# Grouped attention by head pairs and half tokens, the convolution's layer norm behind it, and lo of that stage's weights made by adding transfers

## The chip, the cores and the metric

The kernel runs on one core of a Trainium2 chip. The metric is the device time of one execution in microseconds (us), lower is better. The kernel of before takes 1296.93 us (median of three runs, 1295.86 to 1297.26).

## The reference

Two transformer blocks in float32 on 512 tokens of width 1024. The first has a pooling mixer and a stick-breaking attention with 16 heads. The second, which the change touches, has a mixer of two parallel branches, then cross attention to 256 memory tokens, then a gated feed-forward net. Cut to what matters here:

```python
def parallel_mixer(h, ...):            # h: 512 x 1024
    z = h @ w_in                       # 512 + 512 for the convolution, 512 for q, 128 + 128 for k and v
    a = a_val * sigmoid(a_gate)
    a = silu(layernorm(dwconv_centred(a, conv_dw, conv_dw_b), conv_ln_g, conv_ln_b))   # 31 taps, 512 channels
    q = apply_axial_rope(rmsnorm(q, q_norm_g))    # 8 heads of 64
    k = apply_axial_rope(rmsnorm(k, k_norm_g))    # 2 heads of 64, each for four heads of q
    att = softmax(q k^T / 8) v
    return concatenate([a, att]) @ w_out
```

Behind it stand a residual with its norm, and the cross attention, whose keys and values (`mem_n @ w_mem_kv`) depend on the memory alone.

## The kernel before

**Products in three parts.** Operands are split as x = hi + lo, both float32r, and each product is three matmuls, hi*hi + hi*lo + lo*hi (`mm3`, line 149). A weight tile of 128 x 1024 is loaded from SP's queue into a raw buffer (three of them, line 183), ACT copies it to hi (`wh`) and DVE subtracts to lo (`wl`) (`weights`, lines 186 to 193); wh and wl have four buffers each. Matmuls with plain float32 operands (transposes, products with v, memory keys and values) are single.

**The stage.** `pair(j)` (line 865) makes value and gate of 128 channels of the convolution, `tokens` (line 238) the queries, lines 884 to 894 keys and values. `conv_steps` (line 811) gives DVE 30 taps per channel group, 120 in all, then the layer norm: sums, mean by a matmul, squares, second matmul, scaling. These steps are paced: `catch_up` (line 125) gives out taps as long as DVE's counted time over `CONV_RATE` is behind PE's counted time.

**The attention.** `gqa_scores(n_)` (line 956) makes one head's scores against 512 keys for four blocks of 128 tokens, twelve products with 64 rows of contraction, and its softmax (line 917): maximum on DVE, exponential and sum on ACT, reciprocal on DVE, scaling on ACT. `turn_p` transposes the probabilities on PE, ACT copies them out. After every second head eight products with v give two heads' output (lines 982 to 989). `fill` (line 256) puts steps of the memory keys (`mem_k_steps`) and values (`mem_v_steps`) in between as work for PE. After the loop the rest of the taps and the norm are given out, then follow fillers, the first halves of four tiles of w_out2 with the attention's output (lines 999 to 1005), silu and split of the convolution, and `post_norm` (line 1022) with the second halves. `fill(1000)` at line 1123 gives out the fillers that are left. PSUM has eight banks, all from one pool. Instructions of one engine run in the order in which a compile-time planner lays them out; it starts from the order of the program and moves ahead what is ready.

**For comparison**, the first attention's scores (`score_products`, line 561) alternate the two heads of a pair, whose operands lie in partitions 0 to 63 and 64 to 127; its products with v (`unit_out`, line 622) are 512, 384, 256 and 128 columns wide.

The lines that set the old order, quoted:

```python
        for q in range(4):
            ps = PS("sc")
            qs_ = slice(q * P, q * P + P)
            mm3(ps, qh[r, qs_], ql[r, qs_], kh[r], kl[r], True, True)
```

Of the kernel before, what the change touches and what calls it, by code (L numbers as in the profile page):

```python
# [18 lines left out]
P = 128  # L19
# [12 lines left out]
RATES = (0.5, 0.6)  # L32
TAIL = 1.0
AHEAD = 3
CONV_RATE = 0.87
FILL_A = 2.5
FILL_B = 1.5
FILL_C = 4.0


VEC = {}
# [24 lines left out]
def tile_kernel(ctx: ExitStack, tc: tile.TileContext, A, out):  # L66
# [6 lines left out]
    up_scope = ExitStack()  # L73
    up = up_scope.enter_context(tc.tile_pool(name="up", bufs=2))

    uid = [0]

    def nm(s):
# [14 lines left out]
    def PS(name="ps"):  # L93
        return pp.tile([P, S], F32, tag="ps", name=nm(name))
# [47 lines left out]
    def mm(o, l, r, start, stop):  # L142
        nc.tensor.matmul(o, l, r, start=start, stop=stop, skip_group_check=True)  # L143
# [5 lines left out]
    def mm3(o, lh, ll, rh, rl, start, stop):  # L149
        mm(o, lh, rh, start, False)  # L150
        mm(o, lh, rl, False, False)
        mm(o, ll, rh, False, stop)
        back["pe"] += 3 * o.free_size() / 2400.0
        catch_up()
# [7 lines left out]
    def V(name, j=0):  # L162
        c = VEC[name] + j
        return vec[:, c:c + 1]
# [21 lines left out]
    def weights(src, n=1024):  # L186
        raw = raw_weights(src, n)
        hi = wp.tile([P, 1024], F32R, tag="wh", name=nm("wh"))
        lo = wp.tile([P, 1024], F32R, tag="wl", name=nm("wl"))
        ins = (act(hi[:, :n], raw[:, :n], AF.Copy), tt(lo[:, :n], raw[:, :n], f(hi[:, :n]), ALU.subtract))  # L190
        while before:
            tc.add_manual_dep(ins[len(before) - 1], before.pop(), NOSYNC, reason="order of arrival")
        return hi, lo

    def dense(srcs, xsp):

        KT = len(xsp)
        ws = [weights(src, KT * P) for src in srcs]
        ps = [PS() for _ in srcs]
        for k in range(KT):  # L200
            c = slice(k * P, k * P + P)
            for p_, (wh, wl) in zip(ps, ws):
                mm3(p_, wh[:, c], wl[:, c], xsp[k][0], xsp[k][1], k == 0, k == KT - 1)
        return ps
# [8 lines left out]
    def scaled_weights(src, gain, k0, n):  # L213

        raw = raw_weights(src)
        hi = wp.tile([P, 1024], F32R, tag="wh", name=nm("wh"))
        lo = wp.tile([P, 1024], F32R, tag="wl", name=nm("wl"))
        for i in range(1024 // n):
            c, g = slice(i * n, i * n + n), V(gain, k0 + i)
            act(hi[:, c], raw[:, c], AF.Copy, scale=g)  # L220
            stt(lo[:, c], raw[:, c], g, f(hi[:, c]), ALU.mult, ALU.subtract)
        return hi, lo
# [15 lines left out]
    def tokens(src, gain, xsp, h, mid=None):  # L238

        pv = [PS() for _ in range(4)]  # L240
        for k in range(KD):
            if k % 2 == 0:
                wh, wl = scaled_weights(src[h * 4 + k // 2], gain, k, S) if gain else weights(src[h * 4 + k // 2])
            c = slice(k % 2 * S, k % 2 * S + S)
            for t in range(4):
                tk = slice(t * P, t * P + P)
                mm3(pv[t], xsp[k][0][:, tk], xsp[k][1][:, tk], wh[:, c], wl[:, c], k == 0, k == KD - 1)
                weave(0.68)
            if k == 4 and mid is not None:
                mid()  # L250
        return pv
# [260 lines left out]
    def evac_split(ps, g=None, n=S):  # L512
        hi, lo = G2(n)
        if g is None:
            act(hi, ps, AF.Copy)
            tt(lo, ps, f(hi), ALU.subtract)
        else:
            act(hi, ps, AF.Copy, scale=g)
            stt(lo, ps, g, f(hi), ALU.mult, ALU.subtract)
        return hi, lo  # L520
# [247 lines left out]
    xs, hsp = ple(1, xs, xsp, pl, n4, "mix_pre", mem_normed)  # L768


    mk = []
    mv = [[None, None], [None, None]]


    def mem_k_steps():
        for m in range(KD):
            raw = raw_weights(A["w_mem_k"][m])
            ps = PS()
            for k in range(KD):
                mm(ps[:, :M_MEM], raw[:, k * P:k * P + P], mem[k], k == 0, k == KD - 1)  # L780
                step_pe(0.43)
                yield 0.43
            mk.append(evac_split(ps[:, :M_MEM], None, M_MEM))

    def mem_v_steps(h):
        pv = [PS() for _ in range(2)]
        for kk in range(4):
            raw = raw_weights(A["w_mem_v"][h * 4 + kk])
            for k2 in range(2):
                k = 2 * kk + k2  # L790
                for t in range(2):
                    mm(pv[t], mem[k][:, t * P:t * P + P], raw[:, k2 * S:k2 * S + S], k == 0, k == KD - 1)
                step_pe(1.7)
                yield 1.7
        for t in range(2):
            mv[t][h] = evac_split(pv[t])


    conv = []
# [11 lines left out]
    def conv_steps():  # L811
        for j in range(4):
            while len(conv) <= j:
                yield 0.1
            av, cv = conv[j]
            for kk in range(31):
                d = 15 - kk
                if d == 0:
                    continue
                lo, hi = max(0, -d), min(S, S - d)  # L820
                stt(cv[:, lo:hi], av[:, lo + d:hi + d], V("conv_dw", 31 * j + kk), cv[:, lo:hi],
                    ALU.mult, ALU.add)
                yield 0

        cvs = [c[1] for c in conv]
        acc = G(name="ca")
        tt(acc, cvs[0], cvs[1], ALU.add)
        for j in (2, 3):
            tt(acc, acc, cvs[j], ALU.add)
        yield 3.0  # L830
        psm = PS()
        mm(psm, mean2, acc, True, True)
        acc = G(name="ca")
        for j in range(4):
            tt(cvs[j], cvs[j], psm, ALU.subtract)
            sq = acc if j == 0 else G(name="csq")
            act(sq, cvs[j], AF.Square)
            if j:
                tt(acc, acc, sq, ALU.add)
            yield 0  # L840
        yield 3.0
        psv = PS()
        mm(psv, mean2, acc, True, True)
        RC = rsqrt_(psv)
        yield 1.0
        for j in range(4):
            tt(cvs[j], cvs[j], RC, ALU.mult)
            yield 0

    def rotated(x, t, n, which):  # L850

# [11 lines left out]
        return o  # L863

    def pair(j):
        return dense([A["w_in2"][j], A["w_in2"][4 + j]], hsp)

    back.update(pe=0.0, dve=0.0, rate=CONV_RATE, steps=None)
    p0 = pair(0)
# [13 lines left out]

    pkv = [PS() for _ in range(2)]
    for kk in range(2):
        wh, wl = weights(A["w_kv2"][kk])
        for k4 in range(4):
            k = 4 * kk + k4
            c = slice(k4 * 256, k4 * 256 + 256)
            for t in range(4):  # L890
                o = pkv[t // 2][:, (t % 2) * 256:(t % 2) * 256 + 256]
                tk = slice(t * P, t * P + P)
                xh, xl = hsp[k][0][:, tk], hsp[k][1][:, tk]
                mm3(o, xh, xl, wh[:, c], wl[:, c], k == 0 and t % 2 == 0, k == KD - 1)
# [58 lines left out]
                outs.append(o)  # L953
        return outs

    def gqa_scores(n_):
        j, hd = n_ // 2, n_ % 2
        qh, ql = q2[j]
        r = slice(64 * hd, 64 * hd + 64)
        sc = []  # L960
        for q in range(4):
            ps = PS("sc")
            qs_ = slice(q * P, q * P + P)
            mm3(ps, qh[r, qs_], ql[r, qs_], kh[r], kl[r], True, True)
            sc.append(ps)
        return softmax(sc, S, *(x.rearrange("p (t h) -> p h t", t=4)[:, n_] for x in (qfac[:, :32], nqfac)))

    nqfac = negative(qfac[:, :32], 32)

    queue.append(mem_k_steps())  # L970
    queue.append(mem_v_steps(0))
    att = []
    pts = []
    cur = gqa_scores(0)
    fill(4)
    for n_ in range(8):
        nxt = gqa_scores(n_ + 1) if n_ < 7 else None
        fill(FILL_A)
        pts.append(turn_p(cur, S, False))
        fill(FILL_B)  # L980
        if n_ % 2:
            po = PS("o")
            for i in range(4):
                for hd in range(2):
                    mm(po[64 * hd:64 * hd + 64], v2[:, i * P + 64 * hd:i * P + 64 * hd + 64], pts[hd][i],
                       i == 0, i == 3)
            back["pe"] += 3.6
            catch_up()
            att.append(evac_split(po))
            pts = []  # L990
        cur = nxt

    for _ in back["steps"] or ():
        pass
    back["steps"] = None
    queue.append(mem_v_steps(1))
    fill(FILL_C)

    NW = 4
    wo = [weights(A["w_out2"][m]) for m in range(NW)]  # L1000
    wps = [PS() for _ in range(NW)]
    for m in range(NW):
        for k in range(4):
            c = slice(k * P, k * P + P)
            mm3(wps[m], wo[m][0][:, c], wo[m][1][:, c], att[k][0], att[k][1], k == 0, False)
    csp = []
    for j in range(4):
        c = conv[j][1]
        act(c, c, AF.Silu, scale=V("ln_g", j), bias=V("ln_b", j))
        csp.append(split(c))  # L1010

    def mixed(m):
        if m >= NW:
# [3 lines left out]
            mm3(wps[m], wo[m][0][:, c], wo[m][1][:, c], csp[k][0], csp[k][1], False, k == 3)  # L1017
        return wps[m]

    HALF = [slice(0, S // 2), slice(S // 2, S)]  # L1020

    def post_norm(mk_ps, half_ps, nhalf, gname, xs, done, at=1, ahead=()):

# [81 lines left out]
    def dense_halves(srcs, xsp):  # L1105
# [4 lines left out]
        for h in range(2):  # L1110
            for k in range(KD):
                c = slice(k * P, k * P + P)
                for p_, (wh, wl) in zip(ps, ws):
# [7 lines left out]
    xs = post_norm(mixed, half_steps([A["w_out2"][6], A["w_out2"][7]], att + csp), 2, "mix_post", xs,  # L1121
                   half_split(hsp, "mem_pre"), ahead=[A["w_mem_q"][m] for m in range(AHEAD)])
    fill(1000)


    mo = []
# [255 lines left out]
```

## Time and profile before

| | us |
|---|---|
| median of three runs | 1296.93 |
| the profiled execution | 1295.55 |
| its span, first to last instruction | 1293.8 |
| PE busy | 1273.2 |
| DVE busy | 850.9 |
| ACT busy | 659.0 |
| POOL busy | 4.2 |

Engines are PE (matmuls), DVE (vector), ACT (scalar activations), POOL (GpSimd) and SP (transfers). Times in a view count from the start of the span. Busy times of engines overlap, so they don't add up to the span; a wait on an engine matters only where the chain that ends last runs through it. A matmul's shown length overlaps with the next one's start; the distance between starts is its price. One float32 product appears as two instructions. What lies around the span, 1.75 us here, belongs to the time of the execution.

### The profile page before, as it was taken

The numbers are of one execution on the slowest core, as the hardware profiler recorded it, in microseconds if no ns is written. First come the engines' busy times: TensorE is split into PE (matmuls) and PEld (weight loads), VectorE is DVE, ScalarE is ACT, GpSimd is POOL, SyncE is SP. The second block draws the span as 40 slices with busy tenths as digits, with TensorE's granted clock in tenths as the row PEclk, the third lists the DMA queues.
The fourth block names the chain that finished last, engine by engine and source line by source line (L and its number), as shares of the span: only waits on it lengthen the run. The fifth ranks groups of instructions, "written<-read, shape, count | busy, mean of one in ns | idle before, by whom it ended". The sixth has DMA issues, their size and how long they took to land.

```text
span 1293.8 us, 16129 instructions
## 1 busy us (share of the span) xinstructions
PE 1273.2 (98%) x6228; PEld 1030.6 (80%) x6228; DVE 850.9 (66%) x1369; ACT 659.0 (51%) x1081; POOL 4.2 (0%) x46
## 2 busy tenths in 40 slices
PE   8999999999999999999999999999999999999997
PEld 6888888877777678888777488888988888888886
DVE  6885455587687744869999746543768877773223
ACT  6434344577675543543477755464545544442221
POOL 0000000000000000000000000000000000000000
PEclk9999999999999999999999999999999999999999
DMA  6323234212121243322122243301133333333321
GB/s 230 111 90 120 97 117 133 94 53 79 58 89 37 79 166 99 106 82 82 49 66 65 79 136 111 99 33 70 62 117 98 98 98 96 98 90 105 91 74 65
DMA packets 38957, 120.37 MB, mean 93 GB/s; under 512 B 4448, under 2 KB 8160, under 8 KB 38880
## 3 DMA queue, kind: packets, MB, share of 16 engines
q1 hardware_dynamic: 38880, 119.34, 29.2%
q8 instruction: 49, 0.80, 0.3%
q14 instruction: 28, 0.23, 0.1%
HBM read 115.12 MB, written 4.19 MB: 92 GB/s over the span
## 4 chain that ended last, share of the span: by engine, by line
PE 96%; DVE 2%; ACT 1%; issue 0%; DMA 0%; SPq 0%; DVEq 0%; ACTq 0%
PE ps L143 85%; PE o L143 3%; PE sc L143 3%; PE y L143 2%; PE pT L157 1%; PE aT L157 1%; PE ps L157 1%; DVE z L134 0%; ACT aT L113 0%; ACT hi L113 0%; DVE yg L134 0%; ACT wh L113 0%; DVE og L134 0%; DMA vec<-in_vec_dram 0%; DVE kp L588 0%
## 5 line engine op out<-in xcount | busy, mean ns | idle before, releaser
L143 PE MATMUL ps<-hi,wh 128*128 128x512 f32 (+1 forms) x1390 | 524.6, 378 | 6.2 <-ACT hi L349 5.0
L143 PE MATMUL ps<-lo,wh 128*128 128x512 f32 (+1 forms) x1390 | 519.7, 374 | 0.0
L143 PE MATMUL ps<-hi,wl 128*128 128x512 f32 (+1 forms) x1390 | 518.8, 373 | 0.0
L134 DVE TENSOR_TENSOR wl<-wr,wh 128x1024 fp32r<-128x1024 f32 (+2 forms) x160 | 191.1, 1197 | 179.2 <-ACT wh L113 172.9
L113 ACT ACTIVATE wh<-wr 128x1024 fp32r<-128x1024 f32 (+2 forms) x160 | 165.3, 1039 | 280.5 <-PE ps L143 182.5
L143 PEld LDWEIGHTS ps<-hi,wh 128*128 128x128 f32 x1390 | 262.4, 189 | 55.5 <-ACT hi L349 5.7
L143 PEld LDWEIGHTS ps<-lo,wh 128*128 128x128 f32 x1390 | 262.5, 189 | 47.4 <-DVE lo L350 1.5
L143 PEld LDWEIGHTS ps<-hi,wl 128*128 128x128 f32 x1390 | 262.3, 189 | 46.4 <-DVE wl L134 0.4
L143 PE MATMUL ps<-wh,hi 128*128 128x512 f32 (+1 forms) x256 | 100.4, 392 | 0.0
L143 PE MATMUL ps<-wh,lo 128*128 128x512 f32 (+1 forms) x256 | 96.6, 377 | 0.0
L143 PE MATMUL ps<-wl,hi 128*128 128x512 f32 (+1 forms) x256 | 96.5, 377 | 0.0
L139 DVE SCALAR_TENSOR_TENSOR cv<-aval,vec,cv 128x497 f32<-128x497 f32 (+14 forms) x120 | 84.8, 738 | 1.5 <-ACT cv L113 0.9
L139 DVE SCALAR_TENSOR_TENSOR wl<-wr,vec,wh 128x512 fp32r<-128x512 f32 (+1 forms) x80 | 48.5, 641 | 29.4 <-ACT wh L113 29.3
L139 DVE SCALAR_TENSOR_TENSOR fc<-fu,vec,fc 128x511 f32<-128x511 f32 x88 | 64.4, 748 | 4.0 <-ACT fc L113 2.9
L113 ACT ACTIVATE wh<-wr,vec 128x512 fp32r<-128x512 f32 (+1 forms) x80 | 47.1, 641 | 35.2 <-PE ps L143 22.5
L143 PEld LDWEIGHTS ps<-wh,hi 128*128 128x128 f32 x256 | 48.2, 188 | 10.6 <-issue 2.6
L143 PEld LDWEIGHTS ps<-wh,lo 128*128 128x128 f32 x256 | 48.2, 188 | 9.1
L143 PEld LDWEIGHTS ps<-wl,hi 128*128 128x128 f32 x256 | 48.3, 189 | 7.7 <-issue 0.2
L588 DVE TENSOR_TENSOR_SCAN kp<-kp,begin 128x383 f32<-128x383 f32 (+2 forms) x64 | 49.7, 809 | 6.4 <-ACT kp L113 6.1
L134 DVE TENSOR_TENSOR fu<-ps,R 128x512 f32<-128x512 f32 x44 | 29.4, 686 | 23.3 <-PE ps L143 23.1
L134 DVE TENSOR_TENSOR sq<-sq,sq 128x512 f32<-128x512 f32 (+1 forms) x58 | 38.0, 655 | 5.9 <-ACT sq L113 4.2
L113 ACT ACTIVATE fc<-fu,vec 128x512 f32<-128x512 f32 x44 | 34.7, 809 | 10.4 <-DVE fu L134 10.0
(163 smaller groups left out, 1316.9 us busy)
## 6 DMA issues: line engine op xcount, KB each, us to landing
wr<-in_w_up_dram SPq DMA_DIRECT2D x44, 512.0 KB, 3.5
wr<-in_ple_gate_dram SPq DMA_DIRECT2D x16, 512.0 KB, 3.5
wr<-in_w_down_dram SPq DMA_DIRECT2D x16, 512.0 KB, 3.6
wr<-in_a_w_in_dram SPq DMA_DIRECT2D x14, 512.0 KB, 3.6
wr<-in_a_w_out_dram SPq DMA_DIRECT2D x8, 512.0 KB, 3.5
wr<-in_w_k_dram SPq DMA_DIRECT2D x8, 512.0 KB, 3.6
wr<-in_b_w_q_dram SPq DMA_DIRECT2D x8, 512.0 KB, 3.5
wr<-in_w_v_dram SPq DMA_DIRECT2D x8, 512.0 KB, 3.5
```

The source lines that it names most:

```text
L113: ins = nc.scalar.activation(o, i, fn, **kw).ins
L134: ins = nc.vector.tensor_tensor(o, a, b, op).ins
L139: nc.vector.scalar_tensor_tensor(o, a, s, b, op0, op1)
L143: nc.tensor.matmul(o, l, r, start=start, stop=stop, skip_group_check=True)
L157: nc.tensor.transpose(o, i, ident)
L588: nc.vector.tensor_tensor_scan(o, o, begin[:, :n - 1], 0.0, ALU.mult, ALU.add)
```

## The change

`gqa_scores(j, g)` now does two heads (pair j) for two blocks of tokens (half g), alternating the heads in each of the three parts; one reciprocal serves all four blocks. `gqa_turn` transposes such a unit, `gqa_out` multiplies it with v, 256 columns wide, one unit later, right behind the next scores. The layer norm of the convolution leaves the paced steps and becomes `conv_norm`, with four stops behind the attention. Memory keys and values are first copied out plainly and split later (`mem_split`); three filler steps move from the end of the stage to a new place (`FILL_D`). For the stage's fourteen weights `added_weights` makes lo as -raw on ACT and lets a transfer from POOL's queue add the raw weights from DRAM to it. The taps' pace goes from 0.87 to 0.76.

```diff
-CONV_RATE = 0.87
+CONV_RATE = 0.76
+FILL_D = 4.0
...
+    def added_weights(src, n=1024):
+
+        raw = raw_weights(src, n)
+        hi = wp.tile([P, 1024], F32R, tag="wh", name=nm("wh"))
+        lo = wp.tile([P, 1024], F32R, tag="wl", name=nm("wl"))
+        act(hi[:, :n], raw[:, :n], AF.Copy)
+        act(lo[:, :n], raw[:, :n], AF.Copy, scale=-1.0)
+        nc.gpsimd.dma_start(lo[:, :n], src, accum_op=ALU.add)
+        return hi, lo
...
-            mk.append(evac_split(ps[:, :M_MEM], None, M_MEM))
+            if m % 2 == 0:
+                mk_raw.append(G(name="mkr"))
+            act(mk_raw[-1][:, m % 2 * M_MEM:m % 2 * M_MEM + M_MEM], ps[:, :M_MEM], AF.Copy)
...
+    def mem_split():
+
+        while mk_raw:
+            t = mk_raw.pop(0)
+            for i in range(2):
+                mk.append(split(t[:, i * M_MEM:i * M_MEM + M_MEM], M_MEM))
+        for t, h in list(mv_raw):
+            mv[t][h] = split(mv_raw.pop((t, h)))
...
+    def conv_norm():
+
         cvs = [c[1] for c in conv]
         acc = G(name="ca")
         tt(acc, cvs[0], cvs[1], ALU.add)
         for j in (2, 3):
             tt(acc, acc, cvs[j], ALU.add)
-        yield 3.0
+        yield
...
         psv = PS()
         mm(psv, mean2, acc, True, True)
         RC = rsqrt_(psv)
-        yield 1.0
         for j in range(4):
             tt(cvs[j], cvs[j], RC, ALU.mult)
-            yield 0
+            act(cvs[j], cvs[j], AF.Silu, scale=V("ln_g", j), bias=V("ln_b", j))
+            csp.append(split(cvs[j]))
+        yield
...
     def pair(j):
-        return dense([A["w_in2"][j], A["w_in2"][4 + j]], hsp)
+        return dense([A["w_in2"][j], A["w_in2"][4 + j]], hsp, added_weights)
...
+    def gqa_scores(j, g):
         qh, ql = q2[j]
...
+        sc = [[PS("sc") for _ in range(2)] for _ in range(2)]
+        for q in range(2):
+            qc = slice((2 * g + q) * P, (2 * g + q + 1) * P)
+            for n_, (a, b) in enumerate(((qh, kh), (qh, kl), (ql, kh))):
+                for hd in range(2):
+                    r = slice(64 * hd, 64 * hd + 64)
+                    mm(sc[hd][q], a[r, qc], b[r], n_ == 0, n_ == 2)
...
+        nc.vector.reciprocal(sm, sm)
+        for n_ in range(4):
+            act(pr[n_], pr[n_], AF.Copy, scale=sm[:, n_:n_ + 1])
+        return pr
...
+    def gqa_out(n_, pts):
+        g = units[n_][1]
+        if g == 0:
+            po[0] = PS("o")
+        for i in range(4):
+            for hd in range(2):
+                mm(po[0][64 * hd:64 * hd + 64, HALF[g]], v2[:, i * P + 64 * hd:i * P + 64 * hd + 64],
+                   pts[4 * hd + i][1], i == 0, i == 3)
+        step_pe(1.8)
+        if g:
+            att.append(evac_split(po[0]))
...
     for n_ in range(8):
-        nxt = gqa_scores(n_ + 1) if n_ < 7 else None
+        nxt = gqa_scores(*units[n_ + 1]) if n_ < 7 else None
+        if late is not None:
+            gqa_out(n_ - 1, late)
         fill(FILL_A)
-        pts.append(turn_p(cur, S, False))
+        late = gqa_turn(cur)
         fill(FILL_B)
...
+    csp = []
+    norm_steps = conv_norm()
+    next(norm_steps)
     fill(FILL_C)
+    next(norm_steps)
...
+        if m == 1:
+            next(norm_steps)
+    mem_split()
+    fill(FILL_D)
...
     fill(1000)
+    mem_split()
```

## Rows read from the trace of the kernel before

**Rows 1.** The page: the span, then busy us, share of it and instructions of each engine
```profile
span 1293.8 us, 16129 instructions
...
PE 1273.2 (98%) x6228; PEld 1030.6 (80%) x6228; DVE 850.9 (66%) x1369; ACT 659.0 (51%) x1081; POOL 4.2 (0%) x46
```

**Rows 2.** The page, chain that ended last, shares by engine
```profile
PE 96%; DVE 2%; ACT 1%; issue 0%; DMA 0%; SPq 0%; DVEq 0%; ACTq 0%
```

**Rows 3.** Busy time per stretch: length, engines, clock, DMA share, GB/s
```profile
570.25:638.20 67.95, 67.95 (x355) 58.30 (x355) 64.57 (x140) 25.34 (x41) 0.00 (x0) 1.00 0.25 78
639.40:739.25 99.85, 99.80 (x453) 65.39 (x453) 88.37 (x168) 72.92 (x150) 0.00 (x0) 1.00 0.21 64
```

**Rows 4.** PE's list of waits, 541 to 810: total us, times, longest
```profile
PE sc L143 <- ACT hi L113: 0.7, 1, 0.7
```

**Rows 5.** Chain in order of time, 630 to 800: start us, us, what; first its shares
```profile
by line: PE ps L143 67.2%; PE sc L143 14.4%; PE o L143 9.7%; PE pT L157 8.2%; ACT hi L113 0.4%; PE ps L157 0.3%; issue 0.1%
...
647.38 2.93 PE sc L143 x12
...
666.22 1.00 PE o L143 x2
...
689.34 3.58 PE o L143 x16
```

**Rows 6.** Timeline of PE, first attention's scores: start us, us, what, idle before
```profile
291.90 0.50 PE L143 MATMUL y<-hi,hi 64*128 64x512 f32 x2
...
292.80 0.50 PE L143 MATMUL ps<-wh,hi 128*128 128x512 f32 x1
```

**Rows 7.** Chain in order of time, 340 to 350, first attention's products with v
```profile
344.01 2.30 PE o L143 x16
```

**Rows 8.** Instructions on tile o: ns min/median/max, starts, forms
```profile
L143 PE MATMUL o<-aT,v x128: 272/458/643, 305.9 to 465.8; 128*64 128x512 f32 x32, 128*64 128x384 f32 x32, 128*64 128x256 f32 x32, 128*64 128x128 f32 x32
```

**Rows 9.** Groups on DVE, 570 to 740: count, busy us, mean ns, idle before
```profile
L139 DVE SCALAR_TENSOR_TENSOR cv<-aval,vec,cv 128x497 f32<-128x497 f32 (+14 forms) x120 | 84.8, 738 | 1.5 <-ACT cv L113 0.9
L924 DVE TENSOR_REDUCE mx<-sc 128x1 f32<-128x512 f32 x32 | 21.6, 687 | 3.1 <-PE sc L143 3.1
L134 DVE TENSOR_TENSOR wl<-wr,wh 128x1024 fp32r<-128x1024 f32 x10 | 12.1, 1219 | 5.8 <-ACT wh L113 5.8
...
L134 DVE TENSOR_TENSOR hl<-ps,hl 128x256 fp32r<-128x256 f32 x8 | 3.3, 417 | 0.0
```

**Rows 10.** Timeline of ACT, passes over weights
```profile
546.78 1.06 ACT L113 ACTIVATE wh<-wr 128x1024 fp32r<-128x1024 f32 x1
...
580.56 2.01 ACT L113 ACTIVATE wh<-wr 128x1024 fp32r<-128x1024 f32 x2 [5.75 <-PE ps L143]
...
614.74 1.06 ACT L113 ACTIVATE wh<-wr 128x1024 fp32r<-128x1024 f32 x1 [3.55 <-PE ps L143]
```

**Rows 11.** Groups on POOL, whole span
```profile
L584 POOL MEMSET kp<- 128x2 f32 (+1 forms) x40 | 3.3, 101 | 332.3 <-ACT kp L113 187.3 <-DVE wl L139 104.2 <-DVE kp L588 38.7
```

**Rows 12.** Loads of raw weights (line 183), whole span: issue to landing
```profile
DMA to landing us min/median/max: 2.7/3.5/6.3
```

**Rows 13.** Timeline of PE, first products with three of the weights
```profile
558.37 0.39 PE L143 MATMUL ps<-hi,wh 128*128 128x512 f32 x1
...
592.15 0.39 PE L143 MATMUL ps<-wh,hi 128*128 128x512 f32 x1
...
627.16 0.47 PE L143 MATMUL ps<-hi,wh 128*128 128x512 f32 x1
```

**Rows 14.** Timeline of DVE, the convolution's norm
```profile
729.73 2.48 DVE L134 TENSOR_TENSOR cv<-cv,ps 128x512 f32<-128x512 f32 x4 [2.33 <-PE ps L143]
732.13 2.28 DVE L134 TENSOR_TENSOR ca<-ca,csq 128x512 f32<-128x512 f32 x3
```

**Rows 15.** Timeline of PE, filler at the stage's end
```profile
792.50 7.89 PE L143 MATMUL ps<-wr,in 128*128 128x512 f32 x18
```

**Rows 16.** Timeline of DVE, last slice of the first half
```profile
797.05 0.48 DVE L139 SCALAR_TENSOR_TENSOR lo<-x,vec,hi 128x256 fp32r<-128x256 f32 x1 [0.18 <-ACT hi L113]
```

More of the change, by code (lines that the diff above doesn't have):

```diff
@@ L74, in tile_kernel @@
     up = up_scope.enter_context(tc.tile_pool(name="up", bufs=2))
+    HALF = [slice(0, S // 2), slice(S // 2, S)]
     uid = [0]
@@ L193, in weights, with dense @@
         return hi, lo
-    def dense(srcs, xsp):
+    def added_weights(src, n=1024):
[6 more added lines that the diff above has]
+        return hi, lo
+    def dense(srcs, xsp, weights=weights):
         KT = len(xsp)
@@ L242, in tokens @@
             if k % 2 == 0:
-                wh, wl = scaled_weights(src[h * 4 + k // 2], gain, k, S) if gain else weights(src[h * 4 + k // 2])
+                wh, wl = scaled_weights(src[h * 4 + k // 2], gain, k, S) if gain else added_weights(src[h * 4 + k // 2])
             c = slice(k % 2 * S, k % 2 * S + S)
@@ L768, in tile_kernel @@
     xs, hsp = ple(1, xs, xsp, pl, n4, "mix_pre", mem_normed)
-    mk = []
-    mv = [[None, None], [None, None]]
+    mk, mk_raw = [], []
+    mv, mv_raw = [[None, None], [None, None]], {}
     def mem_k_steps():
@@ L795, in mem_v_steps @@
         for t in range(2):
-            mv[t][h] = evac_split(pv[t])
+            mv_raw[t, h] = G(name="mvr")
+            act(mv_raw[t, h], pv[t], AF.Copy)
+    def mem_split():
[5 more added lines that the diff above has]
+            mv[t][h] = split(mv_raw.pop((t, h)))
     conv = []
@@ L839, in conv_steps @@
                 tt(acc, acc, sq, ALU.add)
-            yield 0
-        yield 3.0
+        yield
         psv = PS()
@@ L844, in conv_steps @@
         RC = rsqrt_(psv)
-        yield 1.0
         for j in range(4):
             tt(cvs[j], cvs[j], RC, ALU.mult)
-            yield 0
+            act(cvs[j], cvs[j], AF.Silu, scale=V("ln_g", j), bias=V("ln_b", j))
+            csp.append(split(cvs[j]))
+        yield
     def rotated(x, t, n, which):
@@ L885, in tile_kernel @@
     for kk in range(2):
-        wh, wl = weights(A["w_kv2"][kk])
+        wh, wl = added_weights(A["w_kv2"][kk])
         for k4 in range(4):
@@ L954, in turn_p @@
         return outs
-    def gqa_scores(n_):
-        j, hd = n_ // 2, n_ % 2
+    def gqa_scores(j, g):
         qh, ql = q2[j]
[L959 to L966, printed above, removed]
+        sc = [[PS("sc") for _ in range(2)] for _ in range(2)]
[5 more added lines that the diff above has]
+                    mm(sc[hd][q], a[r, qc], b[r], n_ == 0, n_ == 2)
+            step_pe(3 * S / 2400.0)
+        pr = []
+        mx, sm = (con.tile([P, 4], F32, tag=t, name=nm(t), bufs=4) for t in ("mx", "sm"))
+        for hd in range(2):
+            c = slice(2 * hd, 2 * hd + 2)
+            scale, nscale = (x.rearrange("p (t h) -> p h t", t=4)[:, 2 * j + hd, 2 * g:2 * g + 2]
+                             for x in (qfac[:, :32], nqfac))
+            for q in range(2):
+                nc.vector.tensor_reduce(mx[:, 2 * hd + q:2 * hd + q + 1], sc[hd][q], AX.X, ALU.max)
+                dve(S)
+            tt(mx[:, c], mx[:, c], nscale, ALU.mult)
+            for q in range(2):
+                n_ = 2 * hd + q
+                e = G(name="sme")
+                act(e, sc[hd][q], AF.Exp, bias=mx[:, n_:n_ + 1], scale=scale[:, q:q + 1], accum_out=sm[:, n_:n_ + 1])
+                pr.append(e)
+        nc.vector.reciprocal(sm, sm)
+        for n_ in range(4):
+            act(pr[n_], pr[n_], AF.Copy, scale=sm[:, n_:n_ + 1])
+        return pr
@@ new lines, in gqa_turn @@
+    def gqa_turn(pr):
+        out = []
+        for hd in range(2):
+            for kt in range(0, 4, 2):
+                ps = PS("pT")
+                for k in range(2):
+                    for q in range(2):
+                        transpose(ps[:, k * 256 + q * P:k * 256 + q * P + P],
+                                  pr[2 * hd + q][:, (kt + k) * P:(kt + k + 1) * P])
+                o = G(name="pT")
+                act(o, ps, AF.Copy)
+                out += [(hd, o[:, :256]), (hd, o[:, 256:])]
+        return out
@@ L972, in tile_kernel @@
     att = []
-    pts = []
-    cur = gqa_scores(0)
+    units = [(j, g) for j in range(4) for g in range(2)]
+    po = [None]
+    def gqa_out(n_, pts):
[3 more added lines that the diff above has]
+        for i in range(4):
+            for hd in range(2):
+                mm(po[0][64 * hd:64 * hd + 64, HALF[g]], v2[:, i * P + 64 * hd:i * P + 64 * hd + 64],
[3 more added lines that the diff above has]
+            att.append(evac_split(po[0]))
+    cur, late = gqa_scores(*units[0]), None
     fill(4)
     for n_ in range(8):
-        nxt = gqa_scores(n_ + 1) if n_ < 7 else None
+        nxt = gqa_scores(*units[n_ + 1]) if n_ < 7 else None
+        if late is not None:
+            gqa_out(n_ - 1, late)
         fill(FILL_A)
-        pts.append(turn_p(cur, S, False))
+        late = gqa_turn(cur)
         fill(FILL_B)
[L981 to L990, printed above, removed]
         cur = nxt
+    gqa_out(7, late)
     for _ in back["steps"] or ():
@@ L1005, in tile_kernel @@
             mm3(wps[m], wo[m][0][:, c], wo[m][1][:, c], att[k][0], att[k][1], k == 0, False)
[L1006 to L1010, printed above, removed]
+        if m == 1:
+            next(norm_steps)
+    mem_split()
+    fill(FILL_D)
     def mixed(m):
@@ L1018, in mixed @@
         return wps[m]
-    HALF = [slice(0, S // 2), slice(S // 2, S)]
     def post_norm(mk_ps, half_ps, nhalf, gname, xs, done, at=1, ahead=()):
```

## The prediction

> **What bounds the kernel now.** I read the busy times first: TensorE (PE) is busy for 1273.2 of the span's 1293.8 us, VectorE (DVE) for 850.9 [rows 1]. Then the chain that ended last: 96% of it is PE [rows 2]. So what counts is PE's own work and the few places where it waits; work on other engines counts only if PE comes to wait for it. Then the stage that the change touches, by stretches: from the second pair of the convolution's inputs to the end of the projections (570.25 to 638.20) PE is busy all the time, and in the attention with its fillers (639.40 to 739.25) for 99.80 of 99.85 us; DVE is busy for 64.57 and 88.37 us there, 91% of the time [rows 3]. PE's list of waits has one entry between 541 and 810 us, 0.7 us [rows 4]. A gain can therefore come only from PE work that goes away, while DVE, close behind, must not fall back when PE gets quicker.
>
> **The scores.** Before, one head's twelve products run one behind the other, 2.93 us for twelve; in the chain of 170 us from 630 to 800 they hold 14.4%, 24.5 us, and the products with v 9.7%, 16.5 us [rows 5]. The change alternates the two heads of a pair, whose operands lie in partitions 0 to 63 and 64 to 127. The first attention already does that: six products of 512 columns, alternating, take from 291.90 to 292.80, 0.90 us [rows 6]. With p for one step and s for the change into and out of this form, 12p + s = 2.93 and 3p + s = 0.90, so p = 0.226 and s = 0.22. Twelve products as six steps cost 6p + s = 1.58 us; eight units cost 12.6 instead of 24.5 us: **11.9 us less**. The range's other end for this step is no pairing at all: 8 x 2.93 = 23.4, 1.1 less.
>
> **The products with v.** They come in eight groups of 256 columns instead of four of 512. Before, a group is 4 x 512 = 2048 columns for 3.58 us [rows 5]; in the first attention a unit has 512 + 384 + 256 + 128 = 1280 for 2.30 [rows 7, 8]. That is 1.67 ns a column and 0.17 us fixed, and shows that widths down to 128 cost no more per column. A new group is 1024 columns: 1.71 + 0.17 = 1.88 us, eight are 15.0: **1.5 us less** than the 16.5 there now. Together 13.4 less. But 8 x 2.93 + 4 x 3.58 is only 37.7, while 41.0 stand in the chain: 3.3 us go where scores and products with v cut each other up (1.00 us for two of v's instructions that run alone, [rows 5]). If the new order is cut up as badly, the gain is 13.4 - 3.3 = 10.1. I take the middle, **11.7**. The sixteen transposes a unit and the fillers keep count and shape: no change.
>
> **lo by adding transfers.** In the fourteen weights of the stage (eight of w_in2, four of w_q2, two of w_kv2) the DVE pass goes, ten of them 12.1 us in the stretch [rows 9]. In its place come a second ACT pass (two together 2.01 us [rows 10]) and a transfer on POOL's queue, which waits for that pass. ACT is given some 14 us more, where it is busy for 25.34 of 67.95 us [rows 3]: hidden. POOL's queue holds nothing else here; its only group of size, forty memsets of kp, belongs to the first attention [rows 11]. SP's queue keeps its loads; the fourteen transfers read 512 KB again, 7 MB in some 80 us, 90 GB/s over the 78 and 64 of the stretches [rows 3].
>
> What such a transfer takes, T, no row shows. A plain load of the same bytes lands after 2.7 to 6.3 us, 3.5 in the median [rows 12]. An adding one also has to read what it adds to; twice the median, 7 us, is my value, because it reads two streams where the load reads one; the ends are 3.5 us and four times that, 14. The Trainium skill (DMA: Bandwidth & Descriptors, Anatomy of one DMA) prices a plain transfer from GpSimd at 2.0 us plus bytes over 436 GB/s, so 3.2 us here, an estimate from that page; by it the sum stays as it is.
>
> How much may T be? A buffer comes free, ACT makes hi, and PE first uses the tile: 546.78 to 558.37, 580.56 to 592.15 and 614.74 to 627.16 [rows 10, 13]. Take off 2.0 us for two passes, and add the steps before the first product with lo (0.2 to 1.1 us): the room for T is 10.0, 9.8 and 11.5 us in these three (the first pair's second tile, the third of w_q2, the last of all); in the third pair's second tile it is by the same count 10.4, and the other ten have 11.5 us or more. With T = 7 none is late: **0**.
>
> **What the relief is for.** PE's stage shrinks by 12 of 168 us. DVE loses the 12.1 us of these passes, the 3.3 us of the memory keys' halves go behind the attention [rows 9], and so do at least the 4.8 us of the layer norm that rows show [rows 14]. That leaves 152.9 - 12.1 - 3.3 - 4.8 = 132.7 us in 156, 85%. By the kernel's own counters (0.06 us + 1 ns per column or so for DVE, shares of 2400 columns a us for PE) taps and the rest sum to 118 us; at a pace of 0.76 the last tap goes out when 155 us of PE are counted, and the loop ends at 158. So no taps are left over at its end. Of itself this gives nothing, since PE did not wait for DVE [rows 4].
>
> **New waits.** Three places. The softmax waits for one reciprocal per unit instead of two, and the bank of the output stays open over two units, so one bank less turns over: 0 up to 0.7 us a unit, the one wait that rows show, 5.6 in all. The norm: from its subtractions to the last sum of squares took 729.73 to 734.41, 4.7 us [rows 14]; now 24 products of w_out2, 5.4 us, stand over it, but two lo passes of 1.2 us may push in: 0 to 1.7. Behind the second sum come the square root, silu and the halves, under 24 more products and three filler steps (12 instructions at 7.89/18 us, 5.3 [rows 15]), 10.7 us: 0 to 4. Three filler steps leave the end of the stage, where 18 instructions fill 7.89 us [rows 15]. PE then starts the memory queries at about 795 (792.50 + 7.89 - 5.3); the last of eight slices is ready at 797.5 [rows 16], and is needed only after seven slices of nine half-wide products, 7 us: 0. I take 1.5 for all three, near the low end, because ACT and DVE have room now, and keep 0 to 11.
>
> **Sum.** -11.7 + 1.5 = **-10.2**, on the profiled execution's 1295.55 us (span 1293.8 and 1.75 around it): 1285.35. The median of the runs, 1296.93, is 1.38 above that execution: **1286.7 us**.
>
> **Rivals.**
> *The transfers are late (slower).* A wait gives its length as room to tiles whose buffer was already free, so waits come in three bunches: first pair, w_q2, third pair, T - 10.0, T - 9.8 and T - 10.4. At T = 16 us that is 48 - 30.2 = 17.8 us, so 1296.93 - 10.2 + 17.8 = 1304.5 us. It turns where 3T - 30.2 = 10.2, at T = 13.5. For it: no transfer of this kind is in the trace, and DVE is busy 91% of the time beside it. Against it: 13.5 is more than twice the slowest plain load [rows 12]. The Trainium skill (SBUF — State Buffer, SBUF: two separate sides) speaks for it: while DVE runs an instruction that takes both of its port pairs, GpSimd cannot write descriptors, and a transfer of 620 ns took 3100. Five times 3.5 us would be 17.5, an estimate by that page. The same page names copies and tensor_scalar as such instructions, and DVE's work here is two-input arithmetic and reductions [rows 9]; so by its own terms the rule would not bite. 14%.
> *The norm holds PE.* If the three places wait for 7 us in sum: -4.7, 1292.2 us. For it: this chain is moved from under the fillers to where one product needs its end. Against: 10.7 us of cover. 13%.
> *The pairs do not form*, because banks come free one at a time and the order in which instructions are laid out splits them: -1.1 - 1.5 + 1.5 = -1.1, 1295.8 us, no change. Against it: the same order of products keeps its pairs together in the first attention [rows 6]. 6%.
> *Better than forecast:* nothing cut up and no waits, below 1284: 2%. The forecast itself, 1284 to 1290: 65%.
>
> **Numbers.** A measurement of this kernel can tell 0.2%, 2.6 us, from no change. Faster: 65 + 13 + 2 = 80%; same 6%; slower 14%. The range, 1282 to 1295 us, takes in the forecast, the norm's rival and the bounds of the cutting up; it leaves out most of the late transfers.
>
> **What would show it.** In the changed profile the scores' share of the chain should be near 12.6 us and the products with v near 15; the unit of scores should read about 1.58 us. PE should have no wait for a transfer in front of w_in2, w_q2 and w_kv2, and POOL's transfers should land within 9 us. The sum is wrong if PE's idle time in the stage grows by more than 3 us, or if a row shows scores of one head running alone.

## The result and the profile after

The changed kernel takes 1288.54 us (median) against 1297.1 us for the kernel before in the same comparison: ratio 0.9933, 95% interval 0.9920 to 0.9946; that is 8.7 us less by the ratio, 8.6 by the medians. One of its four executions fell into a slow state, took 2985.12 us and is left out of the ratio. The forecast was 1286.7, its range 1282 to 1295. The profiled execution took 1288.55 us, its span is 1286.8. The page's busy times and chain, which answer to [rows 1, 2]:

```profile
span 1286.8 us, 16293 instructions
...
PE 1264.1 (98%) x6292; PEld 1029.2 (80%) x6292; DVE 833.9 (65%) x1347; ACT 675.2 (52%) x1107; POOL 16.4 (1%) x60
...
PE 93%; DVE 5%; ACT 2%; issue 0%; DMA 0%; SPq 0%; DVEq 0%; ACTq 0%
```

PE is busy for 9.1 us less (1264.1 instead of 1273.2), as meant, but the span shrank by only 7.0, and DVE now holds 5% of the chain. (By the medians it is more than 7.0, since the part of the kernel ahead of the change took 0.65 us longer in this profile: the statistics' sums start at 570.09, before at 569.44.) The stretches from there to the first scores, then the first and the second part of the attention; behind the length stand the busy times of PE, PE's weight loads, DVE, ACT and POOL, then the granted clock, the transfers' share and GB/s [rows 3]:

```profile
570.10:640.05 69.95, 69.27 (x365) 59.49 (x363) 64.24 (x146) 35.99 (x53) 8.63 (x10) 1.00 0.65 151
640.05:691.60 51.55, 49.76 (x304) 37.70 (x305) 51.36 (x96) 40.77 (x86) 0.00 (x0) 1.00 0.21 62
691.60:730.70 39.10, 38.60 (x211) 24.41 (x209) 14.87 (x30) 26.26 (x56) 0.00 (x0) 1.00 0.23 74
```

PE's waits from 541 to 810 us (in total, how many, the longest), which answer to [rows 4]:

```profile
PE sc L145 <- ACT pT L115: 2.3, 3, 1.3
PE sc L145 <- ACT hi L115: 0.7, 1, 0.7
```

In the first part of the attention DVE is full, 51.36 of 51.55 us, and PE is not; in the second DVE is busy for 14.87 of 39.10 us. The chain between 640 and 700 us says the same:

```profile
by line: DVE cv L141 54.4%; DVE mx L1001 23.0%; ACT sme L115 9.3%; PE sc L145 4.0%; ACT hi L115 1.8%; ACT pT L115 1.6%; DVE mx L136 1.3%; issue 1.2%; DVE aval L136 1.1%; PE ps L145 1.0%; DVE lo L136 1.0%; DVE sm L1009 0.8%; PE o L145 0.6%
```

In this stretch the convolution's taps (cv) and the maxima behind them, not PE, set the time. PE's timeline shows a unit of scores that runs as forecast, and one that doesn't:

```profile
646.55 0.50 PE L145 MATMUL sc<-hi,hi 64*128 64x512 f32 x2
646.89 0.40 PE L145 MATMUL sc<-lo,hi 64*128 64x512 f32 x2
...
647.82 0.39 PE L145 MATMUL sc<-hi,lo 64*128 64x512 f32 x2
648.13 2.86 PE L145 MATMUL ps<-in,wr 128*128 128x256 f32 x12
...
655.20 0.39 PE L145 MATMUL sc<-hi,hi 64*128 64x512 f32 x1
655.43 0.39 PE L145 MATMUL sc<-lo,hi 64*128 64x512 f32 x1
657.15 0.50 PE L145 MATMUL sc<-hi,hi 64*128 64x512 f32 x1 [1.33 <-ACT pT L115]
657.16 0.49 PE L145 MATMUL sc<-hi,lo 64*128 64x512 f32 x1
657.49 0.40 PE L145 MATMUL sc<-lo,hi 64*128 64x512 f32 x1
657.73 0.39 PE L145 MATMUL sc<-hi,lo 64*128 64x512 f32 x1
```

The first goes in pairs (x2) and takes 648.13 - 646.55 = 1.58 us. In the second no bank is free for the other head, since ACT evacuates pT late: two products run alone, PE waits 1.33 us, then two begin together and two more run alone. Of the eight units two run as forecast. One, the first, has two of the fillers' products inside it; in five the two heads come apart in this way, by 0.16 to 1.96 us. Over the attention, the scores' and then the products' with v busy time, PE first, for the changed kernel:

```profile
639.00:745.00 106.00, 16.37 (x96) 9.38 (x96) 19.98 (x32) 25.16 (x64) 1.00 0.24 76
...
639.00:745.00 106.00, 15.80 (x128) 9.41 (x128) 2.74 (x4) 2.41 (x4) 1.00 0.24 76
```

And before:

```profile
639.00:745.00 106.00, 25.24 (x96) 16.80 (x96) 21.56 (x32) 25.97 (x64) 1.00 0.22 66
...
639.00:745.00 106.00, 16.97 (x64) 4.57 (x64) 2.75 (x4) 2.38 (x4) 1.00 0.22 66
```

The adding transfers (the first row counts those of w_in2; the times to landing are of all fourteen):

```profile
L204 POOL DMA_DIRECT2D wl<-in_w_in_dram x8: 862/864/1007, 545.4 to 616.6; - x8
...
DMA to landing us min/median/max: 6.3/7.4/9.4
```

PE waits for none of them: from the statistics' first sum to the first scores it takes 70.0 us in both kernels (to 640.05, before to 639.44).

### The profile page after: what moved, and what is told of

The parts are those of the page before. It is cut to its first block, busy times and chain, and to the rows that moved or that the text cites. A ratio compares the mean times of both kernels' runs of the same rounds, so it can differ in the third digit from the quotient of the medians.

```text
span 1286.8 us, 16293 instructions
## 1 busy us (share of the span) xinstructions
PE 1264.1 (98%) x6292; PEld 1029.2 (80%) x6292; DVE 833.9 (65%) x1347; ACT 675.2 (52%) x1107; POOL 16.4 (1%) x60
## 4 chain that ended last, share of the span: by engine, by line
PE 93%; DVE 5%; ACT 2%; issue 0%; DMA 0%; SPq 0%; DVEq 0%; ACTq 0%
PE ps L145 84%; PE o L145 3%; DVE cv L141 3%; PE y L145 2%; PE aT L159 1%; PE sc L145 1%; DVE mx L1001 1%; PE ps L159 1%; PE pT L159 1%; ACT sme L115 1%; ACT aT L115 0%; ACT hi L115 0%; DVE yg L136 0%; ACT wh L115 0%; DMA vec<-in_vec_dram 0%
## 5 line engine op out<-in xcount | busy, mean ns | idle before, releaser
L136 DVE TENSOR_TENSOR wl<-wr,wh 128x1024 fp32r<-128x1024 f32 (+1 forms) x146 | 174.1, 1195 | 157.8 <-ACT wh L115 151.4
L141 DVE SCALAR_TENSOR_TENSOR cv<-aval,vec,cv 128x501 f32<-128x501 f32 (+14 forms) x120 | 82.8, 740 | 1.5 <-ACT cv L115 1.0
```

Of the source, the lines that this page charges most:

```text
L136: ins = nc.vector.tensor_tensor(o, a, b, op).ins
L141: nc.vector.scalar_tensor_tensor(o, a, s, b, op0, op1)
```

## The experiments

By "loop" I mean from the start of the first scores to the end of the last product with v: 639.44 to 739.31 before, 97.9 us without the norm's four sums (2.0 us) that lay in it, and 640.05 to 730.71 after, 90.7.

**Is the gain the pairing?** The scores issued head by head:

```diff
-            for n_, (a, b) in enumerate(((qh, kh), (qh, kl), (ql, kh))):
-                for hd in range(2):
-                    r = slice(64 * hd, 64 * hd + 64)
+            for hd in range(2):
+                r = slice(64 * hd, 64 * hd + 64)
+                for n_, (a, b) in enumerate(((qh, kh), (qh, kl), (ql, kh))):
```

> The changed kernel, but the twelve products of a unit go head by head again (three of head 0, three of head 1) instead of alternating. Theory (the gain is the pairing of heads; some 4 us of it are lost because DVE is late): a unit costs 2.9 us again instead of 1.58, 8 x 1.35 = 10.8 us more PE work; the slower PE gives DVE time, so up to 4 us of waits go: 1295 to 1299 us. Rival (the gain comes from the work taken off DVE and from the moved layer norm, not from the pairing): 1288 to 1291 us.

1288.83 us, ratio 0.9950 (0.9938 to 0.9963). This says nothing of the pairing: the two heads' products start in pairs again, as PE's timeline of this run shows:

```profile
646.61 0.51 PE L145 MATMUL sc<-hi,hi 64*128 64x512 f32 x2
```

Whether the planner laid them in pairs again, or left the program's order and PE began a product of one head beside one that stands three places ahead of it, this row doesn't say. The unmerged records of the trace speak for the second: in this unit the two starts of a pair lie 10 ns apart; in the changed kernel's unit at 646.55, where pairs stand side by side, they lie 3 or 4 ns apart, and three places of 3 or 4 ns make 10. So this run doesn't show that the planner changed the order.

Next the order was forced, six products of one head and then six of the other:

```diff
+                    ins = mm(sc[hd][q], a[r, qc], b[r], n_ == 0, n_ == 2)
+                    if prev is not None:
+                        tc.add_manual_dep(ins, prev, NOSYNC, reason="head by head")
+                    prev = ins.name
```

> The changed kernel with the scores head by head, held so: every product of a unit is ordered behind the one before it, so the planner cannot alternate heads (in heads_apart it did: that trace shows the two heads' products in pairs again). The relief of DVE (adding transfers, norm and halves moved) stays. Theory now (pairing and relief give their gain only together): scores are busy for 24 to 26 us instead of 16.4, PE's waits of 2.3 us go: 1292.5 to 1296 us. Rival (the relief made the gain, the pairing's time is only waited away): 1287 to 1289.5 us.

1288.95 us, 0.9940 (0.9928 to 0.9953): the rival's time, but not by its mechanism. A unit of this run in PE's timeline:

```profile
647.41 0.50 PE L145 MATMUL sc<-hi,hi 64*128 64x512 f32 x1
647.75 0.40 PE L145 MATMUL sc<-lo,hi 64*128 64x512 f32 x1
647.99 0.39 PE L145 MATMUL sc<-hi,lo 64*128 64x512 f32 x1
648.00 0.62 PE L145 MATMUL sc<-hi,hi 64*128 64x512 f32 x2
648.33 0.52 PE L145 MATMUL sc<-lo,hi 64*128 64x512 f32 x2
648.56 0.51 PE L145 MATMUL sc<-hi,lo 64*128 64x512 f32 x2
648.80 0.39 PE L145 MATMUL sc<-hi,hi 64*128 64x512 f32 x1
...
649.59 2.86 PE L145 MATMUL ps<-in,wr 128*128 128x256 f32 x12
```

Nine rows, not twelve: three of them hold two products each, which overlap, the second beginning 0.12 to 0.23 us behind the first (the first of these rows is 0.62 us long, a product alone 0.39 to 0.50). The unit takes 2.18 us, between 1.58 and 2.93; the scores are busy for 18.94 us, 2.6 more than in the changed kernel, and the 2.3 us of waits for pT are gone. So about half of the pairing is still there, and what it lost came out of PE's waits. To take all of the pairing away, the old attention was put into the changed kernel:

```diff
-    def gqa_scores(j, g):
+    def gqa_scores(n_):
+        j, hd = n_ // 2, n_ % 2
...
-    units = [(j, g) for j in range(4) for g in range(2)]
+    pts = []
+    cur = gqa_scores(0)
```

> The changed kernel with the attention as before (one head of all queries after another, products with v per pair of heads), and with all the rest of the change: adding transfers, the norm behind the loop, the halves of memory keys and values moved, pace 0.76. Theory (PE's work sets the time; relief of DVE alone gives nothing since PE did not wait for DVE): PE does 10 us more than in the changed kernel and waits for nothing, 1295 to 1298 us, no change against before. Rival (the relief made the gain, as the 0.994 of apart_forced could be read): 1288 to 1291 us.

1294.05 us, 0.9976 (0.9966 to 0.9986), by the ratio 3.1 us less than before: nearer to the theory, but not "no change". The attention's new form is thus worth the other 5.6 us of the 8.7. It holds more than pairs (half tokens, narrower products with v, one unit later), but the busy times say where it gains. The scores of this run:

```profile
639.00:745.00 106.00, 24.45 (x96) 17.06 (x96) 21.25 (x32) 26.00 (x64) 1.00 0.23 70
```

In the changed kernel they are 8.1 us less, the products with v 1.2 us more (15.80 against 14.62), and PE waits 2.3 us more: 4.6 us, where the loop falls by 4.7 (95.34 to 90.7). And the pairing alone, in the kernel before:

> The kernel before with the pairing alone: grouped attention by head pairs and half tokens; the layer norm stays in the paced steps, the pace stays 0.87, lo of the weights stays on DVE, the memory keys' and values' halves stay where they were. Theory (DVE sets the attention's length once PE is quicker): DVE has 152.9 us of work in the two stretches and PE now only some 155, so much of the gain is not realised: 1291 to 1295 us. Rival (the pairing gives its gain whatever DVE does, the rest of the change is worth nothing): 1288 to 1290 us.

1295.91 us, 1.0004 (0.9993 to 1.0014): by the ratio nothing, less than either side expected. Its edit is the attention's part of the change's diff and no other. PE's waits from 541 to 810 us:

```profile
PE ps L144 <- DVE ca L135: 4.0, 1, 4.0
PE sc L144 <- ACT pT L114: 2.5, 3, 1.4
PE o L144 <- ACT pT L114: 1.1, 1, 1.1
```

The loop falls to 92.4 us (93.39 with two of the norm's sums), 5.5 less. Then the second sum of the norm, still at its old place, waits 4.0 us for DVE. That leaves some 1.5 us, and the profile has about as much: from the first scores to the end it is 1294.0 - 641.64 = 652.4 us, before 1293.8 - 639.44 = 654.4. This is lost ahead of the edit, where the clock granted to PE is 0.77 from 405 to 420 us, before 1.00; in five of the eleven executions the mean clock is as low as 0.992, at 1298.07 to 1298.61 us, and whether the kernel brings that on is open. Relief alone gives 3.1 us, the attention's form alone nothing by the ratio and at most some 2 us by the profile, both together 8.7: the attention's form is worth 5.6 us where DVE has been relieved and the norm has cover. Of the relief's parts only the adding transfers were tried by themselves, not the norm's place, the pace or the moved halves.

**What relief gives without the pairing.** PE had no wait before but 0.7 us, so 3.1 us surprised me. The products with v of the kernel before, then of relief_alone, in PE's timeline:

```profile
666.15 1.07 PE L143 MATMUL o<-pT,v 128*64 128x512 f32 x2
668.04 1.08 PE L143 MATMUL o<-pT,v 128*64 128x512 f32 x4
669.94 2.79 PE L143 MATMUL o<-pT,v 128*64 128x512 f32 x10
```

```profile
665.55 3.65 PE L145 MATMUL o<-pT,v 128*64 128x512 f32 x16
687.59 3.65 PE L145 MATMUL o<-pT,v 128*64 128x512 f32 x16
```

What was cut up is whole: they are busy for 14.62 us instead of 16.97, and the loop takes 95.34 instead of 97.9. The cuts are PE work that the order makes; no wait shows them.

**The adding transfers by themselves.** Taken out of the changed kernel (`weights` in place of `added_weights` at the three places), and put alone into the kernel before:

```diff
-        wh, wl = added_weights(A["w_kv2"][kk])
+        wh, wl = weights(A["w_kv2"][kk])
```

> The changed kernel, but the fourteen weights of the stage get lo on DVE again, as before, and no transfer adds. Theory (DVE is the engine that holds the attention back): 14 passes of 1.2 us, 17 us more on DVE, ten of them ahead of the attention, so it enters the attention with some 12 us more of taps to do, and the maxima are late in all eight units instead of five: 1290.5 to 1294 us. Rival (DVE is only beside the path, the waits come from banks or from ACT's order): 1287.5 to 1289.5 us.

> The kernel before with the adding transfers for the fourteen weights and nothing else changed. Theory (DVE's relief is worth something only where PE has become faster): no change, 1295.5 to 1298 us. Rival (the 3 us that vector_lo lost are in the passes themselves, wherever they stand): 3 us less, 1293 to 1294.5 us.

Without them the changed kernel takes 1290.25 us, 0.9961 (0.9949 to 0.9974), 0.28% or 3.6 us more by the ratio, which is what the theory asked for (2 to 5.5 more; the median itself lies just under its range, where before is 1295.85). The last tap starts at 715.4 instead of 702.2, the scores are busy for 17.22 us and the products with v for 16.30. In the kernel before they cost 4.3 us, 1301.34 us and 1.0033 (1.0021 to 1.0044), which neither side expected. The loop grows by 3.2 us (103.03 against 99.87) with no wait for pT, and the products are cut up more: scores 26.09, products with v 18.04 us. Why the planner cuts more there was not tried.

**Is it DVE's order?** Each tap in the attention is tied behind the maxima emitted before it, so the planner can't move it ahead:

```diff
+                if peak[0] is not None:
+                    tc.add_manual_dep(ins, peak[0], NOSYNC, reason="place of the tap")
...
+            peak[0] = tt(mx[:, c], mx[:, c], nscale, ALU.mult).name
```

> The changed kernel, but every tap that the program emits in the attention is ordered behind the latest maxima that the program had emitted before it, so that the planner cannot move it ahead. Taps then come 8 to 11 a unit, to the loop's end, and not 10 to 13 in the first five units. Theory (taps run ahead, DVE is full in the first half, maxima and with them ACT and the banks come late): the maxima are done earlier, the split pairs and PE's waits go, 2 to 4 us less, 1284.5 to 1286.5 us; twelve taps now stand behind the last reciprocal, 7.9 us ahead of the norm's first sum, which may give back 0 to 2 us. Rivals (a bank short, or the single reciprocal of a unit): no change, 1288 to 1289.5 us.

1286.85 us, 0.9933 (0.9920 to 0.9945): the mechanism shows, the size doesn't. The scores are busy for 14.49 us instead of 16.37, the loop takes 89.0 us, 1.7 less; but a wait of 1.44 us for the first pT moved to the products with v, and by ratio nothing is gained. Two steps further from there:

```diff
+        fill(2.0 if n_ == 1 else 0)
         if late is not None:
             gqa_out(n_ - 1, late)
-        fill(FILL_A)
+        fill(FILL_A - 2.0 if n_ == 1 else FILL_A)
```

> The run pinned, with 2.0 us of the filler steps of the second unit moved from behind to ahead of the first products with v, where that trace shows PE waiting 1.44 us for the evacuation of pT. Theory (that wait is the last of size in the attention): 1.0 to 1.5 us less than pinned, 1285.3 to 1286 us. Rival (what is taken from behind is missing there, the wait moves to the next transposes): as pinned, 1286.5 to 1287.3 us.

```diff
+        po[0] = PS("o")
         if g == 0:
-            po[0] = PS("o")
+            att.append((G(dt=F32R, name="hi"), G(dt=F32R, name="lo")))
...
+        act(hi, po[0][:, HALF[g]], AF.Copy)
+        tt(lo, po[0][:, HALF[g]], f(hi), ALU.subtract)
```

> The run pinned, with a bank of its own for the output of each half of the tokens, evacuated at once, so that no bank stays open over two units. Theory of the banks (one bank short splits pairs and delays transposes): the scores' busy time falls from 14.5 to near 12.8 us, 0.5 to 1.5 us less than pinned, 1285.3 to 1286.4 us. Rival (ACT, not the count of banks, sets when a bank is free): four more evacuations on ACT and four more on DVE, no gain or 0 to 1 us more, 1286.5 to 1288 us.

pinned_fill: 1287.05 us, 0.9925 (0.9912 to 0.9937). The first and second part of its attention:

```profile
640.75:691.60 50.85, 50.84 (x311) 38.16 (x312) 48.04 (x88) 42.97 (x91) 0.00 (x0) 1.00 0.19 63
691.60:728.94 37.34, 37.31 (x204) 22.60 (x202) 30.68 (x51) 24.39 (x52) 0.00 (x0) 1.00 0.25 74
```

And its chain from 640 to 700 us:

```profile
by line: PE ps L146 47.3%; PE sc L146 21.4%; PE o L146 15.6%; PE pT L160 14.6%; ACT hi L115 1.0%; PE ps L160 0.2%; issue 0.1%
```

DVE is busy for 48.04 of 50.85 us in the first part, no longer all of it, PE for 88.15 of 88.19 us, and the chain is PE's again. This is the state that the change was meant to bring, but for the scores: they are busy for 15.69 us, 13.3 if all pairs were whole, and in three of the eight units (665.30, 685.43 and 706.05) the heads still come apart, though PE's list of waits, which counts from 0.15 us up, has only the 0.7 us in front of the first scores. What splits them there is open. pinned_bank: 1287.45 us, 0.9928 (0.9916 to 0.9941), scores 14.56 us as in pinned: a bank more doesn't help, so the bank that stays open over two units is not what splits the pairs that are left. Then the changed kernel and pinned_fill side by side:

> The changed kernel once more, beside the next one on the same chip. Expected: 0.992 to 0.9945 of before.

> The kernel pinned_fill once more, beside the changed kernel on the same chip. Theory (taps held to the place that the program gives them, and one filler moved ahead of a wait): its profile is 2.6 us shorter than that of the changed kernel from the statistics ahead of the stage to the end, so 1.5 to 2.6 us less in the median. Rival (a profile of one execution is no more than its scatter): within 1 us.

0.9934 (0.9921 to 0.9948) and 0.9917 (0.9904 to 0.9929); medians 1288.22 and 1286.67 us. The gain of 1.55 us lies at the lower end of the theory's range, and the two intervals overlap. Both runs of pinned_fill beat the kernel before clearly and the changed kernel by 0.08 and 0.17%; that is a likely gain of 1 to 2 us, not a settled one.

**How late may the transfers be?** Each was issued twice:

```diff
         nc.gpsimd.dma_start(lo[:, :n], src, accum_op=ALU.add)
+        nc.gpsimd.dma_start(lo[:, :n], src, accum_op=ALU.add)
```

> The changed kernel, with each adding transfer of the fourteen weights issued twice, one behind the other; lo then holds the weights once too often, and nothing else differs. It measures T, the time of such a transfer as PE sees it, against the room I had counted. If T doubles from 7.4 to some 14.5 us, my rule 3T - 30.2 gives 13.3 us more: 1299 to 1302 us, with three bunches of waits in front of the first pair, w_q2 and the third pair. Rival (the room is larger than counted, or waits of one bunch cover those of the next): under 6 us more, 1287 to 1293 us.

1335.92 us, 1.0305 (1.0289 to 1.0321): far beyond both. PE's waits from 541 to 690 us:

```profile
PE ps L145 <- DMA wl<-in_w_in_dram: 28.3, 6, 8.7
PE ps L145 <- DMA wl<-in_w_q_dram: 7.3, 3, 3.4
```

POOL's timeline, where L204 is the first transfer of a tile and L205 the second:

```profile
563.72 0.86 POOL L205 DMA_DIRECT2D wl<-in_w_in_dram  x1 [9.19 <-DMA wl<-in_w_in_dram]
564.25 1.22 POOL L204 DMA_DIRECT2D wl<-in_w_in_dram  x1
572.08 0.86 POOL L205 DMA_DIRECT2D wl<-in_w_in_dram  x1 [6.61 <-DMA wl<-in_w_in_dram]
```

The second transfer waits on POOL for the first to land, and the next tile's first one stands behind it in POOL's order. A tile then takes (668.29 - 552.77) / 13 = 8.9 us of POOL's queue, against (616.62 - 545.44) / 13 = 5.5 us at which tiles come up in the changed kernel. That is a rate, not a delay of each, and it grows with the thirteen tiles that follow: 13 x 3.4 = 44 us, near the 47 to 48 that were lost. By PE's count its waits for transfers are 35.6 us of these. The rest is in part the clock: the share granted is 0.66 from 560 to 575 us, 0.80 from 605 to 622 and 0.71 from 645 to 680, so PE runs there in part at 1.2 instead of 2.4 GHz, in stretches where it is busy for 6.33 of 15, 12.82 of 17 and 22.50 of 35 us; in the changed kernel it is 1.00 from 541 to 810. The run doesn't test my rule 3T - 30.2, which supposed transfers that overlap; that rule stays open.

## Why the prediction was right, and where it was not

**The number** was 1.8 us too low. Of its two terms the work on PE was too large (11.7 us less forecast; PE's busy time fell by 9.1) and the new waits were near (1.5 forecast; PE's idle time grew by 9.1 - 7.0 = 2.1). That the sum came so near is in part luck: relief, which I had put at nothing, took 2.6 us out of the loop, and parted pairs and waits, for which I had 1.5 us, put 5.4 in (both below).

**The scores.** The unit was right (1.58 us), the sum not. I took 11.7 us for scores and products with v, the middle between whole units and units "cut up as badly". relief_alone has a loop without cuts, 95.34 us. From it, whole pairs give 95.34 - 8 x (2.93 - 1.58) + 8 x 1.88 - 4 x 3.58 = 85.3 us, 12.6 less than before; so by this estimate the forecast's upper term of 13.4 was nearly there to be had. The changed kernel takes 90.7. The missing 5.4: 2.3 us of waits; scores 16.37 - 8 x 1.66 = 3.1 over whole pairs (1.66 is the first unit above by the same count of busy time, 646.55 to the end of its last product at 648.21); products with v 15.80 - 8 x 1.95 = 0.2. One of the forecast's own signs of a wrong sum has thus come, scores of one head running alone; the other, more than 3 us of idle time, has not.

**What the relief is for** is the step that failed. I put DVE at 85% over 156 us and the last tap near the loop's end, as the pace of 0.76 says, and concluded that "of itself this gives nothing" and that waits take 1.5 us. On the chip the pace holds nothing back: the planner moves taps ahead, DVE is full to 691.60, the last tap starts at 702.2, 28 us ahead of the loop's end. pinned_fill, where taps stay in place, shows the price, 2.5 of the 5.4 us: the loop takes 88.19 us instead of 90.66, PE's waits for pT are gone, and ACT waits 9.8 us for the maxima instead of 13.5. In the time of the whole kernel that is the likely 1 to 2 us of above. An average over a stretch hid that an engine was full in its first half. And relief is worth 3.1 us where PE waits for nothing: scores and products with v are busy for 0.8 and 2.35 us less, since they are cut up less. Why the planner cuts less there was not tried.

**Adding transfers** were right: T taken as 7, measured 7.4 in the median, the slowest 9.4 (a little over the 9 that I had set as a sign), and no wait. DVE was busy for 64.24 of 69.95 us beside them, and POOL's part was 0.86 us each, 1.01 for the first. The Trainium skill (SBUF — State Buffer, SBUF: two separate sides) lets GpSimd be kept from writing descriptors by DVE instructions in a mode that takes both port pairs; this trace agrees in so far as DVE's two-input arithmetic held up none; the one-input kind (tensor_scalar, 0.9 us from 541 to 640 us) is too little here to show a hold. The 3.2 us estimated for a plain transfer from the Trainium skill (DMA: Bandwidth & Descriptors, Anatomy of one DMA) are less than half of what an adding one took.

**The norm** was right: in the list of waits above none lies behind the attention, where I had kept 0 to 5.7 us for it. That this was worth something I had not said: in pairs_alone the old place costs 4.0 us once PE is quicker.

**The rivals.** Late transfers did not come. That pairs don't form came in part, in five units of eight: for late banks in the three where PE waits 2.3 us for pT; in the other two no wait is listed, and what parted them is not shown.

## What to carry to other kernels

When PE's work in a stage is cut, ask which engine is next full, and in which part of the stage, not on average: here 15% of room over the stage was none in its first half. Parts of a change can't be priced one at a time: here the attention's form and relief gave 0 (at most some 2) and 3.1 us alone and 8.7 together, and the adding transfers, worth 3.6 us in the whole, cost 4.3 alone. A run that orders the program anew need not change what the engine does: here both runs that set the heads apart still had products of two heads side by side. Look at the timeline before you trust what a run was meant to show.

## What was not expected of the hardware

In apart_forced six products of head 0 are laid out ahead of six of head 1, and the timeline has nine rows instead of twelve, three of them double. The rows don't name the head; by the order laid out, three of head 1 ran beside three of head 0 that stand ahead of them, 648.00 to 648.56. If the planner left the order of heads_apart as it was, all pairs of its unit at 646.61 are of that kind. The Trainium skill (TensorE: Matmul & The Clock Gate, Part 3, The mechanism) says that products start strictly in order and only weight loads are pulled ahead; here the measurement differs, unless the trace's starts mislead, and so it does from the sentence ahead that an engine's instructions run in the order laid out. Products on different halves of the rows seem to find their own pairs over a distance of three; no run was made to test this by itself.
